# b's gates as two units of seven block products, after w_proj_b, in a hybrid encoder layer

## The chip, the cores and the metric

One core of a Trainium2 chip runs the whole kernel. Its engines are named as in the profile: PE (matmuls), PEld (the weight loads of PE), DVE (elementwise), ACT (activations and copies), POOL, and SP, which here only issues DMAs. The metric is the device time of one execution in microseconds (us); less is better.

## The reference

One encoder layer on 512 tokens of width 1024, in float32. The part that matters is the merge of two branches:

```python
proj = n @ w_in                                  # n: (512, 1024)
zu, zv = ...                                     # 1024 columns each
gate_a = jax.nn.sigmoid(proj[..., OFF_GA:OFF_GB])
gate_b = jax.nn.sigmoid(proj[..., OFF_GB:])      # 1024 columns
ya = s5_branch(xa, ...)                          # a scan over the tokens, then a GLU (w_glu)
yb = sgu_branch(zu, zv, ...)
merged = gate_a * (ya @ w_proj_a) + gate_b * (yb @ w_proj_b)
h = h + merged @ w_out
```

Behind it come a cross-attention over 256 memory tokens (w_k, w_v, w_q, w_xo) and a SwiGLU FFN (w_gate, w_up, w_down).

## The kernel before

**Numbers.** Every float32 operand is held as a pair of tiles, hi (rounded for PE) and lo (the rest), and each product is three matmuls: hi by hi, hi by lo, lo by hi. The pair is made by `split`: a cast on ACT (L85) and a subtraction on DVE (L86).

**Weights.** They come in blocks of 512 KB. `plan` is the list of all blocks in the order of their use. `next_w` takes the next one, and on the way issues the load of the block three ahead (on SP's queue, L137, tile `wraw`) and the split of the block two ahead (`whi`, `wlo`); each of the three tiles has three buffers. SP issues its DMAs in order; so does ACT, which has a few, and POOL, which issues those that add to what lies there (accumulating DMAs).

**Block products.** `feat` (matmuls at L350) multiplies blocks of 512 by 256 weights with all 512 tokens: 24 matmuls of 512 columns for a block. The later stages of the queries, of the FFN and of w_down use another form: a product of 2x2 blocks of weights (512 rows by 256 columns each) by 2x2 blocks of tokens is made of seven block products instead of eight, on sums of blocks, each of 256 tokens (`product`, L1370: 24 matmuls of 256 columns). The sums of weights for it are made in two ways: in SBUF (`plan_unit`: a load at L175, an accumulating DMA at L181, sums on DVE at L184), or in DRAM, long ahead (`plan_sums`: a copy by SP at L267 and an accumulating DMA by POOL, tiles `qsum` and `dsum`). The places of those sums within the plan are given by hand.

**The scan.** The S5 branch runs beside the matmuls as a program of small steps: `tick` after each block lets it go on, `later` puts a step off. The scan's states are in one tile, `zh`, on DVE (L922). For each of four octets of channels `s5_outputs` copies the states into `ss` (ACT, L952 and L953), makes `py` (PE, L966), a gelu of it (ACT, L972), a transpose `pyt` (L978), and stores the result to DRAM as `yd`, half of the stores issued by SP and half by ACT (L986). The kernels of the scan (`pk`, `ks`, `kd`, `tt`) are spread with DMAs that POOL issues (L843 to L851).

**Around the change.** In this order: a's gates (sigmoid, stored to DRAM as `gad`), the mixing `psv` (L1131), `zu` (gelu at L1144, times `sv` at L1145, split into `yb_hi` and `yb_lo`, which lie in the slots E and D), then b's gates and w_proj_b, a column block of 256 of the one and of the other in turn. Of b's gates the sigmoid goes into `part` (L1155), and the product of w_proj_b is multiplied onto it (L1158). Then the S5 pool is closed (`s5.close()`) and the merge's is opened in its place: `ygt` is loaded from `yd` (L1174) and split, w_glu gives `glu` (L1181, L1183) and its split `ya`, `gat` is loaded from `gad` (L1196), w_proj_a is multiplied with the gates, `part` is added, and w_out follows.

The scheduler keeps each engine's instructions in an order of its own that comes from the order of the program, so a step that is moved in the program moves on all its engines and queues.

Of the kernel before, what the change touches and what calls it, by code (L numbers as in the profile page):

```python
# [17 lines left out]
P = 128  # L18
# [34 lines left out]
def hybrid_layer_kernel(  # L53
# [157 lines left out]
    def plan_queries():  # L211

        for q, n in ((1, 0), (5, 0), (2, 0), (6, 0), (1, 1), (7, 0), (2, 1), (4, 0), (3, 0),
# [6 lines left out]

            plan.append(((w_q, 512 * n, q), [(LOADS, load)], lambda got=got: halves(got.pop("raw"))))

    def plan_units(units, down):


        made = [plan_unit(*u, ordered=i == 1) for i, u in enumerate(units)]
        for i in range(2):
            plan_block(w_gate, 4 * i, 4, FS, 256, place=i + 1)
            plan.append(made[0][i + 1])
        plan_feat(w_up, FS, KD)  # L230
        for i, m in enumerate(made):
            nx = made[i + 1] if i + 1 < len(made) else {}
            between = [nx[1]] if nx else down[:2]
            plan.extend([m[5], m[6]] + between + [m[7]] + ([nx[2]] if nx else []) + [m[4], m[3]])
        plan.extend(down[2:])
# [16 lines left out]
    def plan_sums(places):  # L252


        jobs = []
        for q, first, more in ((5, (0, 0), lambda n: query_block(0, 1, n)), (7, (0, 1), lambda n: query_block(1, 1, n)),
                               (6, None, lambda n: query_block(1, 1, n)), (4, None, lambda n: query_block(1, 0, n))):
            for n in range(2):
                jobs.append((qsum[q, n], qsum[q + (-1 if q == 6 else 2), n] if first is None else query_block(*first, n),
                             more(n)))  # L260
        for q, i, jc, more in ((5, 0, 0, lambda c: down_block(0, 1, c)), (7, 0, 1, lambda c: down_block(1, 1, c)),
                               (6, 1, 1, lambda c: down_sum(5, c)), (4, 1, 0, lambda c: down_sum(6, c))):
            for c in range(CHUNKS):
# [29 lines left out]
    for c0 in range(0, GW, 256):  # L293
        plan_feat(w_in, OFF_U + c0, KD)
    for c0 in range(0, D, 256):
        plan_feat(w_in, OFF_GB + c0, KD)
        plan_feat(w_proj_b, c0, KD)
    for c0 in range(0, SW, 256):
        plan_feat(w_glu, c0, SW // P)
    for c0 in range(0, D, 256):  # L300
# [9 lines left out]
    for i in range(4):  # L310
# [4 lines left out]
    plan_down(w_down, lambda q, c: down_tokens[0](q, c), down_plan)  # L315
    plan_units(UNITS, down_plan)

    plan_sums([(5 + 3 * i, 3) for i in range(12)] + [(40 + 2 * i, 2) for i in range(8)] +
              [(79 + 3 * i, 3) for i in range(3)] + [(116 + 5 * i, 4) for i in range(9)])
    used_w = [0]  # L320

    def next_w(*key):
        i = used_w[0]
        used_w[0] += 1
        assert len(plan[i][0]) == len(key) and plan[i][0][1:] == key[1:] and plan[i][0][0] is key[0]
        for j in range(i, min(i + FAR + 1, len(plan))):
# [115 lines left out]
    def tick(us=5.2):  # L442

        side["now"] += us / 5.2
        run_due()
        side["credit"] = min(side["credit"] + us * side["rate"], us)
        while side["credit"] > 0.0 and side["gen"] is not None:
            try:
                used = next(side["gen"])
            except StopIteration:  # L450
                side["gen"] = None
                return
            if used is None:
                side["credit"] = 0.0
                return
            side["credit"] -= used
# [100 lines left out]
    for t in range(1, NT):  # L557
        load_raw(t - 1)
        nc.sync.dma_start(xt[:, t, :], x[t * P:(t + 1) * P])
    xn_hi, xn_lo = token_slot("xn")  # L560
    xn = (xn_hi, xn_lo)

    def first_rows():
# [587 lines left out]

    part = slot("A", (P, KD, T), F32, "part")

    def gb_evac(m, j, ps):
        nc.scalar.activation(part[:, m - OFF_GB // P, :], ps, AF.Sigmoid)  # L1155

    def pb_evac(m, j, ps):
        nc.vector.tensor_tensor(part[:, m, :], ps, part[:, m, :], ALU.mult)  # L1158
# [123 lines left out]

    K0, K1, T0, T1 = slice(0, 4), slice(4, 8), slice(0, 256), slice(256, 512)
# [75 lines left out]
    def product(ps, u, q, start, ops):  # L1361

        hi, lo = next_w(u[0], u[1], q)
        for j in range(2):
            cs = slice(j * P, (j + 1) * P)
            for k in range(4):
                a = (hi[:, k, cs], lo[:, k, cs])
                b = (ops[q][0][:, k, :], ops[q][1][:, k, :])
                for i, (x, y) in enumerate(((0, 0), (0, 1), (1, 0))):
                    nc.tensor.matmul(ps[:, j, :], a[x], b[y], start=start and j == k == i == 0,  # L1370
                                     stop=k == 3 and i == 2, skip_group_check=True)
        tick(2.7)

    def unit_bank(name):
        return bank(name).rearrange("p (j t) -> p j t", j=2)
# [9 lines left out]
    def kept(x, name):  # L1385
        t = np_.tile([P, 2, 256], F32, tag="ev", name=name, bufs=2)
        nc.scalar.copy(t, x)
        return t

    def minus(x, t):  # L1390
        nc.vector.tensor_tensor(t, x, t, ALU.subtract)
        return t


    pts = {}

# [378 lines left out]
```

## Time and profile before

| | us |
|---|---|
| median of 3 runs | 877.51 (877.4 to 878.01) |
| the profiled execution, its own time | 877.18 |
| its span in the profile | 875.4 |
| mean granted clock of PE, share of full speed | 0.997 |
| PE busy | 862.9 |
| DVE busy | 617.4 |
| ACT busy | 464.1 |

The profile is one execution; the time is that of the whole run with what lies around the span. A line such as L350 is a line of the kernel before. In a group's row the columns are line, engine, operation, tile written, tiles read, shape and count, then busy time, mean nanoseconds of one, and idle time of the engine just before them with what ended most of it. In a tile's row three durations are minimum, median and maximum in nanoseconds. In the timeline a row has start, length and what; in brackets stands the idle time before it and what ended it. In the rows of DMA issues the last number is the median time from issue to landing, in us.

### The profile page before, as it was taken

To read this page: it belongs to the slowest core of one execution; us is meant where nothing else is said; L and a number is where in the kernel's file an instruction comes from. 1 tells how busy PE (TensorE), PEld (TensorE's weight loads), DVE (VectorE), ACT (ScalarE), POOL (GpSimd) and SP (SyncE) were. 2 spreads that over 40 slices of the span, in tenths; PEclk is the share of its full clock that TensorE was granted. 3 is DMA by queue.
4 is the path that set the end of the run, shared out by engine and by line. 5 is a ranking of instruction groups with operands and counts; after the bars stand their busy time and mean duration, and the time that the engine had idled before them with its cause. 6 is when DMAs were issued, how large, how long until landed. Compare 5 with 4: busy or idle time off the path is not lost.

```text
span 875.4 us, 14560 instructions
## 1 busy us (share of the span) xinstructions
PE 862.9 (99%) x5753; PEld 759.9 (87%) x5753; DVE 617.4 (71%) x867; ACT 464.1 (53%) x684; POOL 104.9 (12%) x154
## 2 busy tenths in 40 slices
PE   9999999999999999999999999999999999999996
PEld 6787888887888888889899878999999999888875
DVE  5699679968313258669657646767877768898875
ACT  5544875277434234557557444645545454556663
POOL 1001065103311100110000001001111110000000
PEclk9999999999999999999999999999999999999998
DMA  8358369943759946825687144547788963256672
GB/s 260 112 148 249 78 200 257 248 125 107 205 133 278 263 134 211 270 88 174 196 262 218 52 137 128 145 129 187 178 217 212 233 165 79 82 166 198 194 249 87
DMA packets 112134, 154.34 MB, mean 176 GB/s; under 512 B 13545, under 2 KB 78593, under 8 KB 112002
## 3 DMA queue, kind: packets, MB, share of 16 engines
q1 hardware_dynamic: 93042, 128.27, 45.2%
q0 software_dynamic: 16432, 24.09, 16.6%
q10 hardware_dynamic: 2592, 1.05, 0.5%
q8 instruction: 45, 0.74, 0.3%
q14 instruction: 23, 0.19, 0.1%
HBM read 146.60 MB, written 38.24 MB: 211 GB/s over the span
## 4 chain that ended last, share of the span: by engine, by line
PE 93%; DVE 5%; ACT 1%; issue 1%; POOL 0%; POOLq 0%
PE pf L350 29%; PE pt L350 17%; PE px L1370 12%; PE dx L350 7%; PE pq L1370 6%; PE dq L350 3%; PE pv L1370 3%; PE qx L1370 2%; PE dv L350 2%; PE ptr L511 1%; PE py L966 1%; PE po L350 1%; PE qq L1370 1%; DVE wlo L86 1%; PE pz L902 1%; PE pw L883 1%
## 5 line engine op out<-in xcount | busy, mean ns | idle before, releaser
L86 DVE TENSOR_TENSOR wlo<-wraw,whi 128x1024 fp32r<-128x1024 f32 (+1 forms) x139 | 165.0, 1187 | 110.2 <-ACT whi L85 106.9
L85 ACT CAST whi<-wraw 128x1024 fp32r<-128x1024 f32 (+1 forms) x139 | 142.3, 1024 | 168.2 <-PE pf L350 60.1
L350 PE MATMUL pf<-xn,whi 128*128 128x512 f32 x448 | 140.6, 393 | 0.0
L350 PEld LDWEIGHTS pf<-xn,whi 128*128 128x128 f32 x448 | 83.4, 188 | 17.9 <-issue 1.1
L350 PE MATMUL pf<-xn,wlo 128*128 128x512 f32 x224 | 87.7, 391 | 0.0
L1370 PE MATMUL px<-fn,whi 128*128 128x256 f32 x480 | 83.3, 277 | 0.0
L1370 PEld LDWEIGHTS px<-fn,whi 128*128 128x128 f32 x480 | 72.4, 188 | 0.3 <-ACT u L1630 0.2
L85 ACT CAST whi<-b 128x1024 fp32r<-128x1024 f32 x40 | 42.1, 1053 | 50.5 <-PE px L1370 27.1
L86 DVE TENSOR_TENSOR wlo<-b,whi 128x1024 fp32r<-128x1024 f32 x40 | 49.0, 1224 | 28.0 <-ACT whi L85 28.0
L1370 PE MATMUL px<-fn,wlo 128*128 128x256 f32 x240 | 66.5, 277 | 0.0
L350 PE MATMUL dx<-whi,s 128*128 128x512 f32 x170 | 53.9, 392 | 1.4 <-ACT whi L85 1.0
L1370 PE MATMUL pq<-s,whi 128*128 128x256 f32 x320 | 55.1, 277 | 0.0
L86 DVE TENSOR_TENSOR wlo<-t,whi 128x1024 fp32r<-128x1024 f32 x30 | 36.7, 1225 | 20.1 <-ACT whi L85 20.1
L85 ACT CAST whi<-t 128x1024 fp32r<-128x1024 f32 x30 | 31.6, 1052 | 36.0 <-PE pv L1370 12.6
L350 PEld LDWEIGHTS pf<-xn,wlo 128*128 128x128 f32 x224 | 42.1, 188 | 8.6
L1370 PEld LDWEIGHTS pq<-s,whi 128*128 128x128 f32 x320 | 48.3, 188 | 0.1
L1370 PEld LDWEIGHTS px<-fn,wlo 128*128 128x128 f32 x240 | 45.1, 188 | 0.0
L1370 PE MATMUL pq<-s,wlo 128*128 128x256 f32 x160 | 44.3, 277 | 0.0
L350 PE MATMUL pt<-whi,xn 128*128 128x512 f32 x128 | 42.4, 404 | 0.0
L350 PEld LDWEIGHTS dx<-whi,s 128*128 128x128 f32 x170 | 31.7, 188 | 8.4 <-ACT whi L85 1.2
L350 PE MATMUL dx<-wlo,s 128*128 128x512 f32 x85 | 33.1, 390 | 0.0
L1370 PEld LDWEIGHTS pq<-s,wlo 128*128 128x128 f32 x160 | 30.1, 188 | 0.0
(436 smaller groups left out, 2132.1 us busy)
## 6 DMA issues: line engine op xcount, KB each, us to landing
wraw<-in_w_in_dram SPq DMA_DIRECT2D x36, 512.0 KB, 5.2
dsum<-in_w_down_dram SPq DMA_DIRECT2D x20, 512.0 KB, 6.9
wraw<-dsum SPq DMA_DIRECT2D x20, 512.0 KB, 4.1
b<-in_w_gate_dram SPq DMA_DIRECT2D x15, 512.0 KB, 4.1
b<-in_w_up_dram SPq DMA_DIRECT2D x15, 512.0 KB, 3.9
wraw<-in_w_down_dram SPq DMA_DIRECT2D x15, 512.0 KB, 3.8
dsum<-in_w_down_dram POOLq DMA_DIRECT2D x10, 512.0 KB, 7.6
dsum<-dsum POOLq DMA_DIRECT2D x10, 512.0 KB, 7.7
```

The source lines that it names most:

```text
L85: hi = nc.scalar.copy(dst_hi, src)
L86: lo = nc.vector.tensor_tensor(dst_lo, src, dst_hi.bitcast(F32), ALU.subtract)
L350: nc.tensor.matmul(ps, a[x], b[y], start=start and i == 0, stop=stop and i == 2, skip_group_check=free)
L511: tr = nc.tensor.transpose(ps[:, j, :], src[:, k * P:(k + 1) * P], ident)
L883: nc.tensor.transpose(ps[:, j, :], wt[:, 4 * hf + j, :], ident)
L902: in_order(nc.tensor.matmul(ps[hf, g, :], wt[:, g, hf], x, start=g == 0, stop=True, tile_position=(0, 64 * j), skip_group_check=True))
L966: in_order(nc.tensor.matmul(ps[64 * j:64 * j + 64, r, :], a, b, start=r == k == 0, stop=k == 2, tile_position=(0, 64 * j), skip_group_chec ...
L1370: nc.tensor.matmul(ps[:, j, :], a[x], b[y], start=start and j == k == i == 0, stop=k == 3 and i == 2, skip_group_check=True)
```

## The change

1. w_proj_b is computed first, as a whole (8 blocks); its product is only copied into `part`, by ACT.
2. b's gates follow as two units (columns 0 to 511 and 512 to 1023) of seven products each, in an order that interleaves the two (`ORDER`). A product is 24 matmuls of 256 columns; there are 14, in place of 8 blocks of 24 matmuls of 512.
3. The sums of tokens that four of the seven products read are made on DVE (`gate_sum`, `onto`) and split into the slots D and E, which yb leaves; two of the products read quarters of xn as they are.
4. The sums of weights are made in a tile `gw` of the S5 pool, under the tag of the states (`zh`): for each unit two plain loads into it, two accumulating DMAs on POOL, and two sums on DVE with a plain load of another block. 14 transfers of 512 KB take the place of 8.
5. The epilogue of the gates is a sigmoid on ACT and a multiplication onto `part` on DVE (`gate_put`), with copies (`kept`, `u2s`) and subtractions (`minus`) for the results that are a sum of several products.
6. The places of the sums in DRAM are given anew: four of them lie in the stretch of w_proj_b and the gates where there were six. The slot of xn has its two halves at offsets of their own. `product`, `unit_bank`, `kept` and `minus` stand further up in the file, unchanged.

```diff
+    GATES = [(w_in, OFF_GB), (w_in, OFF_GB + 512)]
+    ORDER = ((1, 0), (2, 0), (5, 0), (6, 0), (1, 1), (7, 0), (2, 1), (5, 1), (6, 1), (3, 0), (7, 1), (4, 0), (4, 1), (3, 1))
...
+            def whole(at, src):
+                return lambda: nc.sync.dma_start(gate_place[0](at), src)
+
+            def make(q=q, i=i, b=b, got=got):
+                t, b11 = (gate_place[0](2 * i + j) for j in range(2))
+                if q in (2, 3):
+                    return halves(got.pop("raw"))
+                ops = halves(b11 if q in (1, 7) else t)
+                if q == 5:
+                    nc.vector.tensor_tensor(t, t, got.pop("raw"), ALU.add)
+                elif q == 6:
+                    nc.vector.tensor_tensor(b11, t, b11, ALU.subtract)
+                    nc.gpsimd.dma_start(t, b(1, 0), accum_op=ALU.add)
+                return ops
+
+            loads = {1: [(5, whole(2 * i + 1, b(0, 0)))], 2: [(LOADS, plain(b(1, 0)))],
+                     5: [(8, whole(2 * i, b(0, 0))),
+                         (6, lambda i=i, b=b: nc.gpsimd.dma_start(gate_place[0](2 * i), b(0, 1), accum_op=ALU.add)),
+                         (LOADS, plain(b(1, 1)))],
+                     3: [(LOADS, plain(b(1, 1)))]}
+            plan.append(((w, c0, q), loads.get(q, []), make, got))
...
     for c0 in range(0, D, 256):
-        plan_feat(w_in, OFF_GB + c0, KD)
         plan_feat(w_proj_b, c0, KD)
+    plan_gates()
...
-    plan_sums([(5 + 3 * i, 3) for i in range(12)] + [(40 + 2 * i, 2) for i in range(8)] +
-              [(79 + 3 * i, 3) for i in range(3)] + [(116 + 5 * i, 4) for i in range(9)])
+    plan_sums([(5 + 3 * i, 3) for i in range(10)] + [(38, 5), (44, 5)] + [(50 + 2 * i, 2) for i in range(7)] +
+              [(85 + 3 * i, 3) for i in range(3)] + [(122 + 5 * i, 4) for i in range(10)])
...
-    xn_hi, xn_lo = token_slot("xn")
+    xn_hi, xn_lo = token_slot("xn", APART)
...
-    def gb_evac(m, j, ps):
-        nc.scalar.activation(part[:, m - OFF_GB // P, :], ps, AF.Sigmoid)
-
     def pb_evac(m, j, ps):
-        nc.vector.tensor_tensor(part[:, m, :], ps, part[:, m, :], ALU.mult)
-
-    for c0 in range(0, D, 256):
-        feat(w_in, OFF_GB + c0, xn, KD, gb_evac)
+        nc.scalar.copy(part[:, m, :], ps)
...
+    gops = {1: xq(K0, T0), 2: xq(K1, T0), 7: xq(K0, T1), 4: xq(K1, T1)}
...
+    def gate_sum(n):
+
+        if n == 0:
+            gsum[3] = quarter("x3")
+            onto(gsum[3], gops[7], ALU.subtract, gops[1])
+        elif n == 1:
+            gsum[1] = quarter("x1")
+            onto(gsum[1], gops[4], ALU.subtract, gops[7])
+            split(*gops[7], gsum[3])
+        elif n == 2:
+            gsum[2] = quarter("x2")
+            for i, x in enumerate(gops[1]):
+                V.tensor_tensor(gsum[2], gsum[2 - (i == 0)], x.bitcast(F32), ALU.subtract)
...
+            gate_tiles.append(s5p.tile([P, 4, 4, 256], F32, tag="zh", name="gw"))
...
+    for n, c0 in enumerate(range(0, D, 256)):
         feat(w_proj_b, c0, yb, KD, pb_evac)
+        gate_sum(n)
+
+    gd, ge = (slot(tag, (P, KD * T), F32R, "gs" + tag.lower()) for tag in "DE")
...
+    split(*gops[5], gsum[1])
+    split(*gops[6], gsum[2])
+    onto(gsum[2], gops[2], ALU.add)
+    split(*gops[3], gsum[2])
...
+    def gate_step(q, i):
+
+        u = GATES[i]
+        if q == 1:
+            gx[i], gv[i] = unit_bank("gx"), unit_bank("gv")
+            product(gx[i], u, 1, True, gops)
+            nc.scalar.copy(gv[i], gx[i])
+        elif q == 2:
+            product(gv[i], u, 2, False, gops)
+            gate_put(i, 0, T0, sigmoid(gv[i]))
...
+    for q, i in ORDER:
+        gate_step(q, i)
     finish_side()
     s5.close()
```

More of the change, by code (lines that the diff above doesn't have):

```diff
@@ new lines, in product @@
+    def product(ps, u, q, start, ops):
+        hi, lo = next_w(u[0], u[1], q)
+        for j in range(2):
+            cs = slice(j * P, (j + 1) * P)
+            for k in range(4):
+                a = (hi[:, k, cs], lo[:, k, cs])
+                b = (ops[q][0][:, k, :], ops[q][1][:, k, :])
+                for i, (x, y) in enumerate(((0, 0), (0, 1), (1, 0))):
+                    nc.tensor.matmul(ps[:, j, :], a[x], b[y], start=start and j == k == i == 0,
+                                     stop=k == 3 and i == 2, skip_group_check=True)
+        tick(2.7)
@@ new lines, in unit_bank, with kept, minus, onto @@
+    def unit_bank(name):
+        return bank(name).rearrange("p (j t) -> p j t", j=2)
+    def kept(x, name):
+        t = np_.tile([P, 2, 256], F32, tag="ev", name=name, bufs=2)
+        nc.scalar.copy(t, x)
+        return t
+    def minus(x, t):
+        nc.vector.tensor_tensor(t, x, t, ALU.subtract)
+        return t
+    xq = lambda ks, ts: (xn_hi[:, ks, ts], xn_lo[:, ks, ts])
+    gops = {1: xq(K0, T0), 2: xq(K1, T0), 7: xq(K0, T1), 4: xq(K1, T1)}
+    def onto(dst, x, op, first=None):
+        for i, part_ in enumerate(x):
+            part_ = part_.bitcast(F32)
+            if i == 0 and first is not None:
+                V.tensor_tensor(dst, first[0].bitcast(F32), part_, op)
+            else:
+                V.tensor_tensor(dst, dst, part_, op)
+        if first is not None:
+            V.tensor_tensor(dst, dst, first[1].bitcast(F32), ALU.add)
@@ new lines, in quarter @@
+    def quarter(name):
+        return np_.tile([P, 4, 256], F32, tag="gain", name=name, bufs=2)
+    gsum = {}
+    def gate_sum(n):
[10 more added lines that the diff above has]
+                V.tensor_tensor(gsum[2], gsum[2 - (i == 0)], x.bitcast(F32), ALU.subtract)
@@ new lines, in hybrid_layer_kernel, with gate_tile @@
+    gate_tiles = []
+    def gate_tile(i):
+        if not gate_tiles:
+            gate_tiles.append(s5p.tile([P, 4, 4, 256], F32, tag="zh", name="gw"))
+        return gate_tiles[0][:, i]
+    gate_place[0] = gate_tile
+    for n, c0 in enumerate(range(0, D, 256)):
+        feat(w_proj_b, c0, yb, KD, pb_evac)
+        gate_sum(n)
+    gd, ge = (slot(tag, (P, KD * T), F32R, "gs" + tag.lower()) for tag in "DE")
+    at_ = lambda t, i: t[:, i:i + 1024].rearrange("p (k n) -> p k n", k=4)
+    gops[6], gops[5] = halves_at(gd, 4, 256, APART), halves_at(ge, 4, 256, APART)
@@ new lines, in hybrid_layer_kernel, with gate_put, sigmoid @@
+    gops[3] = (at_(gd, 2176 + APART[0]), at_(ge, 2048 + APART[1]))
+    split(*gops[5], gsum[1])
+    split(*gops[6], gsum[2])
+    onto(gsum[2], gops[2], ALU.add)
+    split(*gops[3], gsum[2])
+    u2s = np_.tile([P, 2, 2, 256], F32, tag="gain", name="u2s", bufs=2)
+    def gate_put(i, f, ts, src):
+        m = 4 * i + 2 * f
+        V.tensor_tensor(part[:, m:m + 2, ts], part[:, m:m + 2, ts], src, ALU.mult)
+    def sigmoid(src, dst=None):
+        if dst is None:
+            dst = np_.tile([P, 2, 256], F32, tag="ev", name="gs", bufs=2)
+        nc.scalar.activation(dst, src, AF.Sigmoid)
+        return dst
@@ new lines, in hybrid_layer_kernel @@
+    gx, gv, gq = {}, {}, {}
+    def gate_step(q, i):
[7 more added lines that the diff above has]
+            gate_put(i, 0, T0, sigmoid(gv[i]))
+        elif q == 5:
+            gq[i] = unit_bank("gq") if i == 0 else aux("gq").rearrange("p (j t) -> p j t", j=2)
+            product(gq[i], u, 5, True, gops)
+        elif q == 6:
+            product(gx[i], u, 6, False, gops)
+            nc.scalar.copy(u2s[:, i], gx[i])
+        elif q == 7:
+            product(gx[i], u, 7, False, gops)
+            u3 = minus(gq[i], kept(gx[i], "u3"))
+            gate_put(i, 1, T1, sigmoid(u3, u3))
+        elif q == 4:
+            product(gx[i], u, 4, False, gops)
+            gate_put(i, 0, T1, sigmoid(gx[i]))
+        else:
+            product(gq[i], u, 3, False, gops)
+            u2 = minus(gq[i], u2s[:, i])
+            gate_put(i, 1, T0, sigmoid(u2, u2))
@@ L1163, in hybrid_layer_kernel @@
+    for q, i in ORDER:
+        gate_step(q, i)
     finish_side()
@@ L1359, in values @@
             split(ot_hi[:, 2 * hd + dt_, :], ot_lo[:, 2 * hd + dt_, :], ps)
[L1361 to L1375, printed above, removed]
     def query_product(ps, n, q, start=False):
```

20 lines of the change are left out of this document (12 added, 8 removed).

## The prediction

> **What bounds the kernel now.** I read the page first, then the stages (the windows view), then the chain of waits in the stretch that the change touches.
>
> ```profile
> PE 862.9 (99%) x5753; PEld 759.9 (87%) x5753; DVE 617.4 (71%) x867; ACT 464.1 (53%) x684; POOL 104.9 (12%) x154
> PE 93%; DVE 5%; ACT 1%; issue 1%; POOL 0%; POOLq 0%
> ```
> TensorE is busy 99% of the span and holds 93% of the chain that ended last. The windows view (stretch, length, then busy time of PE, PEld, DVE, ACT and POOL, the granted clock, DMA share, GB/s) says where that is strictly so:
>
> ```profile
> 152.00:203.00 51.00, 51.00 (x294) 43.10 (x293) 40.86 (x65) 27.52 (x28) 5.98 (x12) 1.00 0.74 188
> 203.00:260.00 57.00, 56.97 (x476) 46.49 (x476) 24.17 (x27) 28.96 (x36) 19.66 (x38) 1.00 0.58 148
> 260.00:300.00 40.00, 40.00 (x179) 33.13 (x178) 14.36 (x16) 13.49 (x17) 5.61 (x6) 1.00 0.97 276
> 264.70:289.10 24.40, 24.40 (x109) 20.20 (x109) 9.12 (x11) 8.10 (x11) 3.64 (x4) 1.00 0.99 298
> ```
> PE never stands still here, so a microsecond of matmul taken out is a microsecond of span, as long as nothing is late. VectorE has 24.17 of 57 us and 14.36 of 40: there is room. The transfers have little: 0.97 to 0.99 of their time is used from 260 on. The chain in order of time (start, length, piece) gives the prices of matmuls:
>
> ```profile
> 251.69 2.77 PE py L966 x48
> 254.46 5.21 PE pf L350 x22
> 259.68 0.44 PE pyt L978 x4
> 260.11 80.27 PE pf L350 x354
> 439.51 2.72 PE qv L1370 x24
> 442.23 8.16 PE qx L1370 x72
> ```
> A matmul of 512 tokens takes 80.27/354 = 0.2268 us, one of 256 takes 2.72/24 = 0.1133 us, half of it.
>
> **The matmuls.** b's gates are 8 blocks of 24 matmuls of 512 tokens: 192 x 0.2268 = 43.5 us. Two units of seven products are 14 x 24 = 336 matmuls of 256 tokens: 336 x 0.1133 = 38.1 us. The gain is 5.4 us, all of it on PE. w_proj_b keeps its 192 matmuls.
>
> **Work added beside it.** DVE gets 10 sums of tokens, 4 splits of them, 4 sums of weights and 6 more weight splits: 24 operations of 1024 elements. Nearest rows:
>
> ```profile
> L86 DVE TENSOR_TENSOR wlo<-wraw,whi 128x1024 fp32r<-128x1024 f32 (+1 forms) x139 | 165.0, 1187 | 110.2 <-ACT whi L85 106.9
> L85 ACT CAST whi<-wraw 128x1024 fp32r<-128x1024 f32 (+1 forms) x139 | 142.3, 1024 | 168.2 <-PE pf L350 60.1
> L184 DVE TENSOR_TENSOR t<-t,b x20: 1215/1224/1226, 561.0 to 748.4; 128x1024 f32<-128x1024 f32 x20
> L1158 DVE TENSOR_TENSOR part<-pf,part x8: 683/692/692, 232.9 to 307.8; 128x512 f32<-128x512 f32 x8
> ```
> 24 x about 1.2 = 29 us, and 4 subtractions of 0.69 = 3 us beyond the eight products with `part` that there were. ACT gets 10 casts of 1.02 and some copies, about 12 us. In the changed program's order the first sums (x3, x1) fall into the zu stage, where DVE is busy 40.86 of 51, and the scan's last step comes some 10 us later, still ahead of its use; the rest falls into the gates: 14 weight splits, 4 weight sums, the last sums and splits of tokens and the epilogues make 16.7 + 4.9 + 6 + 12 x 0.69, about 36 us of 44. Throughput holds; what remains are single late operands, in order of time:
>
> *The last rows of yb.* Before, b's first gate block stands between zu and the first use of yb; after it doesn't.
>
> ```profile
> 218.45 0.62 ACT L85 CAST yb_hi<-zu 128x512 fp32r<-128x512 f32 x1 [1.02 <-DVE zu L1145]
> 185.56 2.04 ACT L952 COPY ss<-zh 64x1008 f32<-64x1008 f32 x1 [0.45 <-DVE zh L922]
> ```
> In the changed order PE finishes zu at about 203.5 and wants the last yb after one block of w_proj_b (24 x 0.2268 = 5.4), a scan product (2.8), its transposes (0.4) and 7 matmuls (1.6): 213.7. Before, ACT had it only at 218.45. Now zu's last gelu is done ahead of the copies of the states, and ahead of the cast stand the scan product (2.8), its gelu (0.6) and two copies of 2.04: 203.5 + 7.5 = 211.0 at the earliest, with 2 to 3 us for what DVE has queued ahead of the product with `sv`. I take 0; bounds 0 to 2.
>
> *Where the states lay.* The tile for the gates' weights takes the states' slot, so SP holds its loads until ACT has copied the last states, which queue behind the gelu of the second scan product (about 231). SP then issues four weight blocks and two copies of w_down sums at once, 3.1 MB.
>
> ```profile
> 243.25 2.91 ACTq L986 DMA_DIRECT2D yd<-tt  x4
> 246.26 1.05 ACT L85 CAST whi<-wraw 128x1024 fp32r<-128x1024 f32 x1 [3.04 <-DMA wraw<-in_w_in_dram]
> 260.76 1.80 ACTq L986 DMA_DIRECT2D yd<-tt  x4
> 264.03 1.05 ACT L85 CAST whi<-wraw 128x1024 fp32r<-128x1024 f32 x1 [3.30 <-DMA yd<-tt]
> dsum<-in_w_down_dram SPq DMA_DIRECT2D x4, 512.0 KB, 13.5
> ```
> ACT issues half of the scan's stores itself, and in the changed program the four of the second octet wait, one by one, for landings of that burst, the last for the second w_down copy. From 231, that lands after 3.1 MB at 276 GB/s (11.3 us) to the 13.5 of the row: 242.5 to 244.5, with its issue behind the others up to 246. The cast of w_proj_b's seventh block is queued behind it on ACT: cast 1.05 and subtraction 1.2 give 246.7 to 248.2, against PE's need at 246.2. I take 1.2; bounds 0 to 2.5.
>
> *Inside the gates.* A product lasts 2.72 us, its weights cost ACT 1.02 and DVE 1.19. The first split into yb's slot has to wait for yb's last reader and is wanted by the third product; slack 0.1 to 0.5 us. I take 0.3; bounds 0 to 2, for 14 products in which DVE is full to 82%.
>
> *The merge.* Call the start of the gates T0, about 257.8 (before's 307.6, when glu began, less 5.4 and less 44.4 for the gates and the scan product that lies in them). The second unit's weight tile is added to by an accumulating DMA that may start only after product 6's split, about T0+28.8.
>
> ```profile
> t<-in_w_gate_dram POOLq DMA_DIRECT2D x5, 512.0 KB, 7.1
> dsum<-in_w_down_dram POOLq DMA_DIRECT2D x3, 512.0 KB, 9.9
> ygt<-yd SPq DMA_DIRECT2D x4, 256.0 KB, 7.4
> gat<-gad SPq DMA_DIRECT2D x4, 512.0 KB, 13.9
> wraw<-dsum SPq DMA_DIRECT2D x4, 256.0 KB, 2.5
> 266.28 0.82 SPq L1174 DMA_DIRECT2D ygt<-yd  x2
> 279.88 0.62 ACT L85 CAST yg_hi<-ygt 128x512 fp32r<-128x512 f32 x1 [1.59 <-DMA ygt<-yd]
> 307.58 0.39 PE L350 MATMUL pf<-yg_hi,whi 128*128 128x512 f32 x1
> ```
> It lands 7.1 later, T0+35.5 to 35.9; cast and subtraction make T0+37.8, and only then are S5's tiles released and the merge's opened in their room. Before, ygt was loaded at 266.28 and split by 280.5, 27 us ahead of glu at 307.58. After, it is issued at T0+37.9 = 295.7, 6.5 us ahead of glu (T0+44.4 = 302.2), and behind it on SP stand a w_down copy, three gat and w_proj_a. If ygt lands in 2.5 (the row for 256 KB on a free queue) glu starts on time; with 7.4 it starts about 2.5 late. [...]
> The later need is proj_a's: T0+56.0 (glu is 48 x 0.2268 = 10.9 and 0.7 of the scan's). ACT's cast of w_proj_a's second block is queued ahead of the casts of ya. Up to that block SP moves 4 x 0.26 + 0.52 + 3 x 0.52 + 2 x 0.52 = 4.2 MB, and POOL 0.5 beside it. At full share the rows give 188/0.74 = 254 to 298/0.99 = 301 GB/s: 15.6 to 18.5 us, T0+53.5 to 56.4. With the cast (1.05) and the last splits of ya (0.62 + 0.62 + 0.69) PE can start at T0+56.5 to 59.4: 0.5 to 3.4 late, I take 2.0. A wait at glu is no addition: PE would then only reach the same landing later.
>
> Behind proj_a the same work follows; one more w_down sum lies in w_out's stage and one in the FFN. I cost that at nothing: the share of DMA time is lower there, and it is work that only w_down reads, at the end:
>
> ```profile
> 341.00:434.00 93.00, 93.00 (x527) 81.10 (x526) 68.54 (x95) 51.74 (x85) 6.41 (x10) 1.00 0.58 188
> 546.00:876.00 330.00, 320.83 (x2356) 301.92 (x2355) 255.51 (x279) 179.18 (x230) 23.75 (x23) 0.99 0.61 167
> ```
> Should that cover be gone, one copy of 6 to 7 us in front of a weight load would cost up to that; I see no place for it at 0.6.
>
> **Sum.** -5.4 + 1.2 + 0.3 + 2.0 = -1.9 us. The profiled execution has its span of 875.4 and 877.18 around it, 0.33 under the median of 877.51; the difference is put on the median: 875.6 us.
>
> **Rivals.**
> *Full cover.* The burst runs at 301 GB/s and the stores are not held up: no stall, -5.4, 872.1. For it: PE rode through 0.99 of DMA share from 264.7 to 289.1 without a gap. Against: there ygt and proj_b were asked for 20 to 40 us ahead, now 6. Chance 0.17.
> *My forecast*, stalls of 2 to 5 us, 0.43: 873.5 to 877.5.
> *The release comes late: slower.* Place: the accumulating DMA of the second unit, and the burst that waits for its reader. If it lands in 9.9 us (the row from the crowded stretch) instead of 7.1, everything behind is 2.8 late, and at 254 GB/s another 1.5: 4.3 over my middle, so -1.9 + 4.3 = +2.4, 879.9. It decides for slower once the last reader of the gates' weights ends later than T0+41.5, 3.7 behind my value, or as much is lost in the burst. For it: all of this is issued in series, each waiting for the last. Against: POOL's queue is otherwise light (5.61 of 40). Chance 0.27.
> *DVE paces the gates.* If each product waits 0.2 to 0.5 us for a split behind a sum, 14 times make 3 to 7: near 877.5, instead of the 0.3 above. Against it stands the 36 of 44 us; for it, that sums and splits share one queue in a fixed order. Chance 0.12.
> *Half the columns are not half the time.* If a matmul were bound by its weight load, 336 loads at
>
> ```profile
> L1370 PEld LDWEIGHTS px<-fn,whi 128*128 128x128 f32 x480 | 72.4, 188 | 0.3 <-ACT u L1630 0.2
> ```
> would be 63.2 us in place of 43.5: about 20 slower, 897. Against it: the 72 matmuls in 8.16 us, with loads overlapping. [...] Chance 0.01.
>
> **How the numbers follow.** A difference under 0.2%, 1.75 us, can't be told from none. Faster by more: all of full cover, 0.24 of my forecast's 0.43, 0.02 of DVE's: 0.43. Same: 0.18 of mine, 0.07 of the late release, 0.06 of DVE's: 0.31. Slower: 0.20, 0.04, 0.01 of mine and 0.01: 0.26. Range 872.3 to 880.3: it reaches from next to full cover to past the late release; my own case alone is 873.5 to 877.5.
>
> **What would show it.** Right: 14 pieces of about 2.72 us in the gates; ygt issued some 6 us ahead of glu, after the last split of the gates' weights; PE idle at proj_a's start, released by a cast of ya behind a landing of w_proj_a; a gap of about 1 us in w_proj_b's seventh block, released by ACT's cast. Wrong: gaps between the products (DVE's rival); no idle PE from 203 to proj_a (full cover); products longer than 2.8 us; a gap at glu longer than the one at proj_a; or time lost behind proj_a, which I have at nothing.

## The result: 1.4% slower

The changed kernel takes 889.28 us (median of 6 runs, 887.58 to 893.05), the one before 877.45 (6 runs): a ratio of 1.0141, interval 1.0114 to 1.0169, 11.8 us. I had forecast 875.6 with a range to 880.3. The profiled execution is the slowest of the six, 893.05; its ledger below ends 3.8 us over the median.

The page of the changed kernel, busy time and chain:

```profile
span 891.3 us, 14922 instructions
PE 867.9 (97%) x5897; PEld 766.6 (86%) x5897; DVE 646.0 (72%) x895; ACT 478.1 (54%) x706; POOL 111.2 (12%) x158
PE 85%; DMA 8%; DVE 2%; ACT 2%; issue 1%; SPq 0%; POOLq 0%; POOL 0%; ACTq 0%; DVEq 0%
```
PE holds 85% of the chain where it held 93%, and DMA 8% where it had none. And PE is *busier*, 867.9 against 862.9, though it has 5.4 us less to multiply: matmuls have become longer. Both have to be explained. The chains of the kernel before (first two lines) and after (last two) say where to look (start, length, piece):

```profile
152.29 7.14 PE psv L1131 x64
340.38 17.01 PE pt L350 x75
```
```profile
155.21 7.14 PE psv L1171 x64
356.40 17.00 PE pt L390 x75
```
From the mixing to w_out the one before takes 188.1 us, the changed one 201.2: 13.1 more, where 5.4 less was due. From w_out to the end of the span they take 535.0 and 534.9. So all of it but 2.9 us lies between, and those 2.9 lie ahead of the mixing.

What PE waited for between 200 and 345 in the changed kernel (us in total, times, longest):

```profile
PE pf L390 <- ACT ya_hi L85: 3.2, 1, 3.2
PE pf L390 <- ACT whi L85: 2.9, 1, 2.9
PE py L1006 <- DMA tt<-kd: 2.0, 1, 2.0
PE gx L1207 <- ACT u L1216: 0.6, 1, 0.6
PE pf L390 <- DVE wlo L86: 0.5, 1, 0.5
PE pf L390 <- DVE ya_lo L86: 0.3, 1, 0.3
```
9.5 us, all but 0.6 of it in three places. Two I had named, at w_proj_b's seventh block (2.9 and 0.5) and at proj_a (3.2 and 0.3); the one at `py`, the scan's last product, I had not. The windows view of the same stretch (PEclk is the third number from the end):

```profile
230.00:260.00 30.00, 26.55 (x172) 20.56 (x169) 10.77 (x10) 11.44 (x13) 11.11 (x19) 0.94 0.86 213
260.00:280.00 20.00, 19.41 (x159) 17.57 (x157) 11.60 (x11) 9.77 (x13) 12.04 (x19) 1.00 0.94 221
280.00:300.00 20.00, 18.57 (x169) 18.27 (x170) 10.03 (x11) 13.04 (x16) 1.18 (x1) 0.91 0.72 170
320.00:341.00 21.00, 17.44 (x69) 13.57 (x68) 13.43 (x16) 8.35 (x13) 3.41 (x3) 0.92 0.99 293
```
The granted clock was 1.00 throughout this stretch before. Now it is 0.94, 0.91 and 0.92 in just the windows that hold the three waits. In the trace's clock records these are three stretches of 3.41 us at half clock (granted 0.50, from 255.08, 282.39 and 333.59), each beginning 1.0 to 1.5 us behind the end of a wait (2.9 to 253.76, 2.0 to 281.43, 3.2 to 332.06): 3 x 1.7 = 5.1 us of full speed gone (the rounded shares of the windows give 5.3).

How the first and second wait came about (timeline; ACT, SP and POOL, brackets: idle before and what ended it):

```profile
237.32 14.81 ACTq L1026 DMA_DIRECT2D yd<-tt  x4
252.66 1.05 ACT L85 CAST whi<-wraw 128x1024 fp32r<-128x1024 f32 x1
241.48 16.26 SPq L1026 DMA_DIRECT2D yd<-tt  x4
266.53 2.41 POOL L308 DMA_DIRECT2D dsum<-in_w_down_dram  x2 [2.30 <-issue]
267.98 4.18 POOL L891 DMA_DIRECT2D tt<-kd  x6
272.87 0.53 POOL L891 DMA_DIRECT2D tt<-kd  x1 [0.72 <-DMA dsum<-in_w_down_dram]
276.20 0.53 POOL L891 DMA_DIRECT2D tt<-kd  x1 [2.80 <-DMA dsum<-in_w_down_dram]
281.43 0.44 PE L1006 MATMUL py<-tt,u 128*64 128x128 f32 x4 [2.02 <-DMA tt<-kd]
```
ACT stands 14.81 us in the issue of its four stores and only then casts the block that PE wants. POOL issues w_down's accumulating DMAs ahead of the scan's `tt`, and two of `tt` wait until one of those has landed; the scan's product waits for them.

And the merge (SP, then ACT, then two rows of DMA issues between 300 and 335):

```profile
311.56 1.77 SPq L1333 DMA_DIRECT2D ygt<-yd  x4
318.45 8.02 SPq L137 DMA_DIRECT2D wraw<-in_w_proj_a_dram  x3
330.45 1.04 ACT L85 CAST whi<-wraw 128x1024 fp32r<-128x1024 f32 x1 [4.62 <-DMA wraw<-in_w_proj_a_dram]
wraw<-in_w_proj_a_dram SPq DMA_DIRECT2D x4, 512.0 KB, 9.6
ygt<-yd SPq DMA_DIRECT2D x4, 256.0 KB, 3.0
```
`ygt` lands 3.0 us (the median of its four blocks) after its issue, glu starts without a wait at 317.8, and the second block of w_proj_a is what comes late. That part went as I had it.

### The profile page after: what moved, and what is told of

The parts are those of the page before. It is cut to its first block, busy times and chain, and to the rows that moved or that the text cites. A ratio compares the mean times of both kernels' runs of the same rounds, so it can differ in the third digit from the quotient of the medians.

```text
span 891.3 us, 14922 instructions
## 1 busy us (share of the span) xinstructions
PE 867.9 (97%) x5897; PEld 766.6 (86%) x5897; DVE 646.0 (72%) x895; ACT 478.1 (54%) x706; POOL 111.2 (12%) x158
## 4 chain that ended last, share of the span: by engine, by line
PE 85%; DMA 8%; DVE 2%; ACT 2%; issue 1%; SPq 0%; POOLq 0%; POOL 0%; ACTq 0%; DVEq 0%
PE pf L390 23%; PE pt L390 17%; PE px L1207 12%; PE pq L1207 6%; PE dx L390 5%; PE dq L390 3%; PE pv L1207 3%; PE qx L1207 2%; PE dv L390 2%; PE gx L1207 2%; DMA wraw<-in_w_proj_a_dram 1%; PE po L390 1%; PE qq L1207 1%; DVE wlo L86 1%; PE py L1006 1%; PE ptr L551 1%
## 5 line engine op out<-in xcount | busy, mean ns | idle before, releaser
L86 DVE TENSOR_TENSOR wlo<-wraw,whi 128x1024 fp32r<-128x1024 f32 (+1 forms) x135 | 160.1, 1186 | 99.2 <-ACT whi L85 98.7
L85 ACT CAST whi<-wraw 128x1024 fp32r<-128x1024 f32 (+1 forms) x135 | 137.9, 1022 | 142.6 <-PE pf L390 39.6
L390 PE MATMUL pf<-xn,whi 128*128 128x512 f32 x320 | 101.7, 397 | 0.0
L390 PEld LDWEIGHTS pf<-xn,whi 128*128 128x128 f32 x320 | 59.6, 188 | 14.4 <-issue 0.4
L390 PE MATMUL pf<-xn,wlo 128*128 128x512 f32 x160 | 63.3, 396 | 0.0
L390 PEld LDWEIGHTS pf<-xn,wlo 128*128 128x128 f32 x160 | 30.0, 188 | 7.1
L390 PEld LDWEIGHTS pt<-whi,xn 128*128 128x128 f32 x128 | 25.0, 200 | 5.9 <-ACT xn L85 0.7
```

The costliest lines, as they stand in the source:

```text
L85: hi = nc.scalar.copy(dst_hi, src)
L86: lo = nc.vector.tensor_tensor(dst_lo, src, dst_hi.bitcast(F32), ALU.subtract)
L390: nc.tensor.matmul(ps, a[x], b[y], start=start and i == 0, stop=stop and i == 2, skip_group_check=free)
```

## The experiments

Two theories stood against each other at first. One: the time goes into waits for operands that the units' weights and the sums' DMAs delay, each wait followed by a stretch at half clock. The other: the order (w_proj_b first) delays the scan and yb, whatever the gates are made of. Beside them stood the offsets of xn, since the matmuls that read it had grown longer.

| kernel | median us | ratio to before | waits of PE from 200 to 345, us |
|---|---|---|---|
| changed | 889.28 | 1.0141 (1.0114 to 1.0169) | 9.5 |
| changed, xn without offsets | 886.88 | 1.0119 (1.0103 to 1.0135) | 10.3 |
| before, xn with offsets | 881.24 | 1.0046 (1.0033 to 1.0059) | none |
| before, order alone | 877.10 | 0.9998 (0.9988 to 1.0007) | none |
| changed, stores by SP | 886.90 | 1.0106 (1.0087 to 1.0125) | 7.9 |
| changed, w_down sums put off | 882.81 | 1.0065 (1.0053 to 1.0077) | 4.9 |
| both | 881.70 | 1.0052 (1.0037 to 1.0066) | 3.4 |
| both, no offsets, sums from w_out on | 884.23 | 1.0082 (1.0070 to 1.0095) | 3.2 |
| the same, first weight sum on DVE | 879.50 | 1.0039 (1.0024 to 1.0054) | 0.7 |
| the same, second too | 881.60 | 1.0050 (1.0034 to 1.0065) | 0.7 |
| first on DVE, w_down sums spread | 878.38 | 1.0012 (0.9996 to 1.0028) | 0.7 |
| first on DVE, w_down sums spread anew | 875.45 | 0.9971 (0.9957 to 0.9985) | 0.7 |
| gates' sums made in DRAM | 889.27 | 1.0128 (1.0115 to 1.0141) | 4.5 |
| before, one wait made by hand | 881.82 | 1.0046 (1.0033 to 1.0059) | 2.2 |

**The offsets of xn, taken out of the one and put into the other.**

```diff
-    xn_hi, xn_lo = token_slot("xn", APART)
+    xn_hi, xn_lo = token_slot("xn")
```


> The changed kernel with the two halves of xn at their old places (no offsets). Theory: the offsets slow the matmuls that read xn (480 of 512 columns take 233 ns in the changed kernel's trace, 227 before). By it those go back to 227 ns, 480 x 6.3 = 3.0 us, with up to 0.9 us in the products that read xn: 885.3 to 886.3, against 889.3. Rival: the offsets are innocent and the slower spacing is a state of PE that something earlier sets: spacing stays at 233 and the time at 889.

> The kernel before with the offsets for xn and nothing else. Theory: the 672 matmuls of 512 columns that read xn take 233 ns in place of 227, 672 x 6.3 = 4.2 us: 881.7. Rival (innocent offsets): 877.5.

The same 96 matmuls in the chains of the kernel before with offsets and of the changed one without:

```profile
161.51 22.40 PE pf L350 x96
```
```profile
160.89 21.77 PE pf L390 x96
```
233.3 ns against 226.8, and this follows the offsets and nothing else. With them the kernel before loses 0.46%, 4.0 us of the 4.2 expected. Without them the changed kernel has its 227 ns back, but gains only 2.4, and the intervals of the two ratios overlap: its profile shows 5.1 us at `py` in place of 2.0, so an edit elsewhere moves the waits too. In the gates the offsets help: without them three products that read xn take 119.7 ns a matmul (8.62/72 in the last placement's chain below), with them 113.3 to 118.2 in the changed kernel.

**The order alone.**

```diff
     for c0 in range(0, D, 256):
-        feat(w_in, OFF_GB + c0, xn, KD, gb_evac)
         feat(w_proj_b, c0, yb, KD, pb_evac)
+    for c0 in range(0, D, 256):
+        feat(w_in, OFF_GB + c0, xn, KD, gb_evac)
```


> The kernel before with w_proj_b ahead of b's gates, which stay 8 blocks of 24 matmuls of 512 columns; copies into part and a multiplication behind the sigmoid. No units, no sums, no tile in the states' slot, the sums for w_down at their old places. Theory (the loss comes from what the units bring: the loads held for the states' slot, the accumulating DMAs, the late release of the S5 tiles): no gap over 1 us, 877 to 878.5. Rival (the order itself, since yb and the scan's products are wanted earlier): gaps of 2 us and over between w_proj_b's blocks remain, 880 to 884.

Ratio 0.9998. PE is busy in 57.00 of 57:

```profile
203.00:260.00 57.00, 57.00 (x476) 46.80 (x476) 22.33 (x24) 24.05 (x34) 19.66 (x38) 1.00 0.59 148
```
The order costs nothing; the rival falls. What I had bounded at 0 to 2 for the last rows of yb is 0 here and in the changed kernel, and 0.7 in the kernels that have the units and no offsets.

**ACT's stores, and w_down's sums.**

```diff
-            (nc.sync, nc.scalar)[l % 2].dma_start(ydo[l], y[C * l:C * l + C])
+            nc.sync.dma_start(ydo[l], y[C * l:C * l + C])
...
-    plan_sums([(5 + 3 * i, 3) for i in range(10)] + [(38, 5), (44, 5)] + [(50 + 2 * i, 2) for i in range(7)] +
+    plan_sums([(5 + 3 * i, 3) for i in range(8)] + [(50 + 2 * i, 2) for i in range(7)] + [(64 + 4 * i, 3) for i in range(4)] +
```
The first edit is the first kernel, the second the second, both the third.

> The changed kernel with all stores of the scan's result issued by SP, none by ACT. Theory (ACT, held by the stores of the second octet, casts w_proj_b's seventh block late): the gap of 2.9 and 0.5 us there goes, and with it the stretch at half clock behind it, which costs 1.7: 884 to 885. Rival (the block would be late anyway, by its own landing or because SP's queue is now held instead): 888 to 891, with a gap of 2 us or more at the same block or the next.

> The changed kernel with the four w_down sums that lie in w_proj_b's and the gates' stretch put off to the key and value products. Theory (POOL's queue, in which accumulating DMAs for w_down stand ahead of the scan's tt, makes the last scan product late; the copies lengthen the burst behind the states' slot): the gap at py goes, the one at w_proj_b's seventh block shrinks below 2, the one at proj_a stays: 883 to 886. Rival (the accumulating DMAs of the gates' weights alone hold POOL and the burst): gap at py and time unchanged, 888 to 890.

> Both: w_down sums put off, and all stores of the scan's result issued by SP. Theory: no gap is left before the merge, only the one at proj_a (3 us and 1.7 of half clock) and the slower xn matmuls: 879 to 882. Rival (SP, now with all stores, is late with the gates' loads; or the scan's tt is late through the gates' own accumulating DMAs): a gap of 2 us and over ahead of the merge, 884 to 888.

The waits of PE between 200 and 345, of these three in turn:

```profile
PE py L1006 <- DMA tt<-kd: 7.3, 1, 7.3
```
```profile
PE py L1006 <- DMA kd<-ks: 3.1, 1, 3.1
PE gx L1207 <- ACT whi L85: 1.2, 2, 0.8
```
```profile
PE py L1006 <- DMA kd<-ks: 2.7, 1, 2.7
```
With the stores on SP the wait at w_proj_b's seventh block is gone, and what was hidden behind it shows: the scan's last product now waits 7.3 us for `tt`. So that block was late through ACT, as I had it, but taking the wait away gave 2.4 us only (886.90, between its two ranges; the intervals overlap), since POOL's queue makes the scan's product later by more. Putting off four w_down sums gave 6.5. Both together gave 7.6, and left 2.7 at `py`. With the sums put off, alone or with the stores, it is no longer the last scan product that waits but the third of four, for `kd`. I had expected a wait at proj_a and none at `py`, and it is the other way round: the second block of w_proj_a is in time in all three kernels (0.6 to 0.7 us are left at proj_a), and the gates' own accumulating DMAs still stand in POOL's queue ahead of the scan's `kd` and `tt`.

**No accumulating DMA for the units' first sum.** The first kernel here adds to both edits above that xn has no offsets and that eleven w_down sums lie from w_out on; the second loads the block of the first sum like any other and adds it on DVE; the third does so with the second sum (`q in (5, 6, 4)`, and a load for product 4):

```diff
-              [(50 + 2 * i, 2) for i in range(7)] + [(64 + 4 * i, 3) for i in range(4)]
+              [(57 + 2 * i, 2) for i in range(11)]
...
+                if q in (5, 6):
+                    nc.vector.tensor_tensor(t, t, got.pop("raw"), ALU.add)
                 ops = halves(b11 if q in (1, 7) else t)
...
-                         (6, lambda i=i, b=b: nc.gpsimd.dma_start(gate_place[0](2 * i), b(0, 1), accum_op=ALU.add)),
```


> The last but the gates in DRAM's forerunner (w_down sums out of the way, stores by SP) with two more edits: xn without offsets, and the w_down sums begin only in w_out's stage, so that none lies in glu's and proj_a's. Theory: the xn matmuls give 2.9 back, less 0.6 in the gates; the 0.5 MB copy and the addition less ahead of w_proj_a take the 1.2 there away; the gap at py (2.65 and 1.7 of half clock) stays, as it comes from the gates' accumulating DMAs: 877.5 to 879. Rival (the py gap was w_down's after all, by what is left of it in the queues): 873.5 to 875.5.

> The same, and the first sum of weights of each unit is no accumulating DMA: the block is loaded like any other and added on DVE, two operations of 1.22 us more. Theory (accumulating DMAs for the gates' weights stand ahead of the scan's kd and tt in POOL's queue): the gap at py goes, with its half clock: 873.5 to 875.5, 0.3% below the kernel before. Rival (DVE, now at over 85% in the gates, is late with weight splits): gaps between the products, 877 to 880.

> The same with the second sum of each unit on DVE too: no accumulating DMA in the gates at all, two more operations of 1.22 us. Theory (the S5 tiles are released late because the last accumulating DMA can only start after product 6's split and takes 7 us): ygt is issued some us earlier against glu and no wait is left at proj_a: 872.5 to 875. Rival (DVE is full): slower than the kernel with one sum on DVE by 1 us or more.

The first of these three keeps the accumulating DMAs, and the wait at `py` (2.5 us). In the second it is gone and one wait of 0.7 is left in the stretch; 884.23 to 879.50 is 4.7 us, the wait and an estimated 1.7 of half clock behind it (as behind each of the three in the changed kernel) with a little over. In the second's chain the mixing and w_out begin here:

```profile
151.27 7.14 PE psv L1170 x64
336.23 19.73 PE pt L389 x87
```
That is 185.0 us from the one to the other, 3.1 less than before. The second sum on DVE as well leaves the stretch as it is (185.1), and `ygt` is issued no earlier (296.2 in both), so its theory falls. At 881.60 it is 2.1 slower, though the two intervals overlap, and no wait between the products shows for it; in its profile the time lies outside the stretch, ahead of the mixing and behind w_out, and why stays open. The first of the three, at 884.23, lies above both its ranges, and the second and third above their theories; the reason stands behind the merge, in the windows of the kernel with one sum on DVE:

```profile
380.00:410.00 30.00, 30.00 (x244) 29.18 (x243) 27.51 (x41) 22.26 (x37) 7.72 (x7) 1.00 0.87 233
410.00:434.00 24.00, 20.99 (x89) 15.82 (x88) 13.57 (x14) 10.97 (x13) 3.40 (x3) 1.00 1.04 291
```
I had put eleven w_down sums there, from w_out on. The transfers use 0.87 of their time, then all of it, and PE stands still for 3 of 24 us.

**The w_down sums, spread.** Two placements, differing in nothing else:

```diff
-[(57 + 2 * i, 2) for i in range(4)] + [(85 + 3 * i, 3) for i in range(3)] + [(112 + 5 * i, 4) for i in range(17)]
+[(65 + 4 * i, 3) for i in range(3)] + [(85 + 3 * i, 3) for i in range(3)] +
+[(95 + 2 * i, 2) for i in range(5)] + [(105 + 5 * i, 4) for i in range(13)]
```


> As the kernel with one sum of weights on DVE, but only four w_down sums in w_out's stage, three in the queries' and the other seventeen in the FFN, one to five blocks. Theory: up to the end of proj_a that kernel was 3.2 us ahead of the one before, and lost it from 400 to 480, where transfers filled the time and weight splits came late; with the sums out of there it keeps 3 us: 873 to 875.5. Rival (the FFN's stages then lack the transfers' time, or the queries are late for another reason): 876.5 to 880.

> As the one with seventeen w_down sums in the FFN, but none in w_out's and w_down's own stages: three in the keys' and values', three in the queries', five in the output projection's, thirteen in the FFN. That kernel was 3.2 us ahead at the end of proj_a, 1.4 after the queries (a wait of 1.4 in w_out) and 2 behind at the end (small waits for splits in w_down's stage). Theory (all of that is where the w_down sums stand): 3 us stay, 874 to 875.5. Rival (it only moves to the next stage that is short of transfers): 876.5 to 879.

The first is even with the kernel before (1.0012), the second beats it: 875.45 against 878.45 in the same runs, ratio 0.9971, interval 0.9957 to 0.9985. Its profiled execution is the slowest of the twelve, 879.19. The chain of that one, with the mixing, three pieces of the gates, w_out and two pieces of the queries:

```profile
152.12 7.14 PE psv L1170 x64
273.45 8.56 PE gx L1206 x72
288.10 2.49 PE gx L1206 x22
293.09 8.62 PE gx L1206 x72
337.10 7.93 PE pt L389 x35
432.01 2.83 PE qx L1206 x24
474.88 2.72 PE qq L1206 x24
```
185.0 us in place of 188.1, as in the kernel with one sum on DVE (185.0) and in the first placement (184.9): the units do bring 3.1 us in their stretch, with one wait of 0.7 left, and the placements change only what is lost behind it. They do not bring 5.4, because most matmuls of the gates take 8.56/72 = 118.9 and 119.7 ns here, where I had priced 113.3: 336 x 5.5 is 1.8 us. Behind w_out this execution takes 540.3 us, where the one before takes 535.0; how much of that the median run of 875.45 loses no trace shows.

**The units' weight sums made in DRAM, long ahead.** The fourteen blocks are then loaded like any other.

```diff
+                nc.sync.dma_start(got["raw"], gate_block(*GSRC[q], n) if q in GSRC else gsums[q, n])
```


> The units keep their products, their order and their sums of tokens, but the four sums of weights of each unit are made in DRAM long ahead, as for the queries, and loaded like any block; no tile in the states' slot, no accumulating DMA and no sum of weights on DVE in the gates; xn without offsets; the queries' and w_down's sums at later places. Theory (the loss is all in how the weights' sums get into SBUF): no gap over 1 us from w_proj_b to w_out, and the 5.4 us of the products show, less about 1.5 for products at 118 ns a matmul: 872.5 to 875. Rival (DVE's extra work or the denser weight stream of 512 KB in 2.72 us is not carried): gaps between products, 877 to 882.

Neither: 889.27. The S5 tiles are released early now, so the merge's loads start in the middle of the gates, and PE waits for weights there:

```profile
275.00:290.00 15.00, 14.24 (x118) 13.94 (x117) 10.14 (x12) 9.30 (x15) 1.20 (x1) 1.00 1.01 348
```
```profile
PE gx L1186 <- ACT whi L85: 2.6, 1, 2.6
PE gx L1186 <- DVE wlo L86: 1.2, 2, 0.8
```
DMA is full at 348 GB/s for 15 us, and gates that take 512 KB in 2.7 us cannot do without it. From the mixing to w_out it takes 192.6 us, 4.5 more than before; the rest of the loss lies in the later stages, to which I had moved the other sums. That the merge's loads are what delays the gates' weights is read from the order of SP's queue; no run moves those loads alone.

**One wait by hand in the kernel before.**

```diff
+        if m == 0:
+            nc.vector.scalar_tensor_tensor(ygt[:, 0, :], part[:, KD - 1, :], 0.0, ygt[:, 0, :], ALU.mult, ALU.add)
```


> The kernel before, with one wait made by hand: the first block of ygt gets 0 times the last row of part added on DVE, so that glu can only start behind a multiplication, an addition and a split after w_proj_b's last matmul. Same numbers come out. Theory (a gap of 2 us or more makes a stretch of 3.41 us at half clock behind it): a gap of 2.2 to 3, and 1.7 more than the gap in time: 881.4 to 882.2. Rival (the half clock has other causes): the gap alone, 879.7 to 880.5, and no stretch at half clock there.

The timeline and the window around it:

```profile
309.11 2.07 PE L350 MATMUL pf<-yg_hi,whi 128*128 128x512 f32 x4 [2.16 <-ACT yg_hi L85]
310.98 0.63 PE L350 MATMUL pf<-yg_lo,whi 128*128 128x512 f32 x1
```
```profile
308.00:313.00 5.00, 3.89 (x11) 3.08 (x12) 2.14 (x3) 0.62 (x1) 0.00 (x0) 0.66 0.31 105
```

The wait is 2.16 us, the four matmuls behind it take 2.07 in place of 0.9, and the granted clock is 0.66 over 5 us: 5 x 0.34 = 1.7 us gone. The time is 881.82 against 877.77 in the same runs, 4.05 more: the wait and 1.9. So this wait of 2.16 us cost 4.05.

## Why the prediction was wrong

The forecast was a loss of 3.5 us against a gain of 5.4. By size the term that failed most is the clock behind the waits, 5.1 us that I had put at nothing; in mechanism it is POOL's queue, which I had called light. Step by step, with what stood in its place in the changed kernel's profile:

- **The matmuls, -5.4.** The count was right, the price too low. I took 113.3 ns from the queries' products; most of the gates' take 118 (`gx`, 45 in 5.32 us in the row below), which makes the gain about 4. In the last placement most take 119, and the gain from the mixing to w_out is 3.1. The chain of the kernel before held a second price for products of this shape, and I took the lower (the first two rows below: 2.83/24 = 117.9 ns, 5.44/48 = 113.3). Nor is 113.3 fixed for the queries: in the last placement's chain above, with their code unchanged, they take 117.9 at 432.01 (2.83/24) and 113.3 at 474.88 (2.72/24). What switches between the two no run told. Where the operand lies counts beside it: without offsets three products that read xn's slot take 119.7 in the last placement (8.62/72), and others 113.2 (2.49/22). (They are four of each unit's seven: products 1, 2 and 4 read quarters of xn as they are, three and not the two that point 3 of the change names, and product 7 reads a sum that is split into xn's slot.)
- **The offsets of xn, not in my sum at all.** They stood in the diff, and I read past them. They cost 480 x 6.5 = 3.1 us, of which 192 matmuls lie behind the mixing (1.2 us) and the rest ahead of it, where they make an estimated 288 x 6.5 = 1.9 us of the 2.9 us of delay there.
- **Where the states lay, +1.2 with 2.5 at most: 3.4.** The mechanism was as told (ACT, four stores, w_proj_b's seventh block), the size not. I let ACT wait until 246 and it waited until 252, 3 of which are the delay that was there already. I began the burst at the gelu, where it began behind the copies of the states that follow it, 4.1 us on; and I put the landings of w_down's copies at 13.5 at most but left out the two accumulating DMAs of the gates' weights, which run in the same burst.
- **`py`, not in my sum: 2.0 here, up to 7.3 with the stores on SP.** In mechanism this is the step that failed most. I wrote of POOL's queue that it was light, by its busy time (5.61 of 40 us). What counted was what the instruction at the head of the queue waits for (`tt` up to 2.80 us for a w_down sum to land), and busy time doesn't hold that. The runs show it: with w_down's sums put off the last product is in time and the third waits instead (3.1, or 2.7 and 2.5 with the stores on SP), and with the first sum of weights on DVE as well neither waits.
- **Inside the gates, +0.3: 0.6.** Near in size by luck: PE waited for a copy on ACT (`u`, L1216), not for the split into yb's slot that I had named. DVE was no bound, and my rival on it fell.
- **The merge, +2.0: 3.5.** Right in place and mechanism, at my upper end of 3.4; the middle that I took was too low. `ygt` was issued 6.2 us ahead of glu (I had 6.5) and landed in 3.0. My sum has nothing for a wait at glu, which no trace from before shows: its rows had 2.5 and 7.4 for landings of 256 KB. In the changed kernel it was 3.0, with a w_down copy, `gat` and w_proj_a issued behind `ygt` on SP, and glu did not wait.
- **The clock, not in my sum: +5.1.** By size this is the term that failed most. I priced every wait at its length. In the changed kernel's trace each of the three waits of 2.0, 2.9 and 3.2 us is followed by 3.41 us at half clock, and the wait of 2.16 made by hand by the same 1.7 us lost (0.66 over 5 us).

The rows for the matmuls (the kernel before, then the changed one):

```profile
575.67 2.83 PE pq L1370 x24
592.35 5.44 PE pq L1370 x48
```
```profile
289.42 5.32 PE gx L1207 x45
```
Together, from the mixing to w_out: -4 (products at 118), +1.2 (offsets), +9.5 (waits), +5.1 (clock), which is 11.8 of the 13.1 measured; the other 1.3 I can't place. Ahead of the mixing 2.9, of which an estimated 1.9 are offsets; the rest, and two stretches at half clock in the first 50 us, may be chance: in single profiles the granted clock over those 50 us is 0.93 here and in the kernel before with offsets, 0.97 with the order alone and in the last placement, and 1.00 in the kernel before, by my estimate two such stretches, one and none; and the kernel with both edits, offsets and all, begins its mixing at 151.70.

Of the rivals, "the release comes late" named the side, slower, but with a mechanism that was not the one that decided: the accumulating DMA of the second unit landed in 7.9 us, 0.8 over my value. "Half the columns are not half the time" is refuted as I put it (118 against 227), though 4% of it was there. The chance of 0.26 for slower was too small: I had four waits in series in my own list, each with an upper end, and took the middle of each or less. At the upper ends, 2 + 2.5 + 2 + 3.4 against 5.4, they alone make +4.5, without any clock.

## What to carry to other kernels

An operand that comes late for a PE that is never idle costs its wait and can cost the clock behind it: here the wait of 2.16 us made by hand cost 4.05, and a wait of 1.4 left the clock at 1.00. A price read off one row can be one of two (113.3 and 117.9 ns here): look for the same product elsewhere in the trace. In the queue of an engine that issues DMAs look at what each instruction ahead waits for (an accumulating DMA that waits for a copy, a store that waits for a burst), not at how busy the engine is; and when one wait is taken away, look for the next one behind it before the gain is counted. A saving in matmuls that needs more bytes has to be paid for with transfers moved out of its stage: here the same units went from 1.4% slower to 0.3% faster with w_down's sums elsewhere, the stores on one queue, the first sum of each unit on DVE in place of an accumulating DMA, and xn where it was.

## What the runs showed of the hardware

- The half clock. In the changed kernel's clock records waits of PE of 2.0, 2.9 and 3.2 us behind the mixing are each followed by 3.41 us at a granted clock of 0.50, and so is one of 1.86 that ends at 25.04 (0.50 from 26.39). Behind the wait of 2.16 made by hand the clock is 0.66 over 5 us, 1.7 us lost; in the stretch with the wait of 2.7 (both edits) 0.95 over 36 us, 1.8 lost. In the stretches with waits of 2.6 (gates' sums in DRAM: 0.85 over 10 us, then 0.84 over 12), 3.1 (w_down sums put off: 0.77 over 15) and 7.3 (stores by SP: 0.83 over 20) twice that is lost, 3.4 to 3.5 us, an estimated 6.8 to 6.9 at half clock. A wait of 1.4 (the kernel with one sum on DVE) left it at 1.00 from 341 to 546. In the changed kernel's records the stretches begin whole multiples of 3.413 us apart: 27.31 us, 8 of them, lie between the first and the second behind the mixing, 51.20, 15 of them, between the second and the third. What decides whether a wait is followed by half clock, and by how much, no run told.
- Offsets of 48 and 112 elements for the two halves of an operand made its matmuls of 512 columns 2.9% longer (226.8 to 233.3 ns), in two kernels. Those of 256 columns in the gates that read it took 119.7 ns without offsets (8.62/72, the last placement) and 113.3 to 118.2 with them (the changed kernel).
- Matmuls of 256 columns, of one shape and from unchanged code, took 113.3 ns in some stretches and 117.9 in others at a granted clock of 1.00, within one execution (the kernel before, 5.44/48 from 592.35 and 2.83/24 from 575.67) and between kernels (the queries: 8.16/72 from 442.23 before, 2.83/24 from 432.01 in the last placement). What decides it stays open.
